# Gate sums beside the output gate tiles only, and the sums of a scan's outputs ten steps later

## The chip, the cores and the metric

The kernel runs on one core of one Trainium2 chip. The metric is the device time of one execution in microseconds. A core has a matrix engine (TensorE, PE in the profile; its weight loads are shown as PEld), VectorE (DVE), ScalarE (ACT), GpSimd (POOL) and a queue engine that issues most transfers (SyncE, SP). Each takes its instructions in the order in which the program gives them, and they wait for each other through semaphores.

## The reference

One decoder layer in float32 for 512 tokens of width 2048: a normalised and conditioned input `h`, one wide projection of it, and two branches that are merged under sigmoid gates. The change lies in the second branch, gated DeltaNet, and in the gate of the conditioning:

```python
mod = jax.nn.silu(c) @ w_ada + b_ada
shift, scale, gate = jnp.split(mod[:, None, :], 3, axis=-1)
...
d_qkv = causal_conv_silu(d_qkv, conv_w)
dq, dk, dv = jnp.split(d_qkv, [DN_KEY, 2 * DN_KEY], axis=-1)
...
o = gated_delta_rule(dq, dk, dv, g, beta)
o = rms_norm(o, dn_norm_w) * jax.nn.silu(dz.reshape(B, T, DN_V_HEADS, DN_HEAD_V).astype(f32))
y_b = o.reshape(B, T, DN_VAL).astype(x.dtype) @ w_o_dn
...
return x + gate * (y @ w_out)
```

There are 16 key heads and 32 value heads, so each key head serves a pair of value heads.

## The kernel before

Float32 products are made of three matmuls: each operand is split into a high part (`hh`, `whi`) and a rest (`hl`, `wlo`), and `mm3` (L250 to L256) adds high by high, rest by high and high by rest. Weights come from memory as `raw` tiles of 1 MB, one per tile of 128 output channels. ScalarE casts half of a tile to `whi` (L52) and VectorE subtracts it to get `wlo` (L53). `channel_tile` runs the 48 matmuls of one such tile, 128 channels by 512 tokens, and calls `pump` after every six of them, eight times in a tile. `pump` is the clock of everything else: a step of each running generator (`live`), of slow paced work, and of side queues, whose entries hold a rate; a side queue adds its rate at every step and moves on by one when it has reached 1. A generator that yields a number sleeps for so many steps. A scheduler then places the instructions on each engine; side work made with `ordered` may not stand before the matmul last issued.

The stage touched is the one of the heads (`heads`, called 16 times by `deltanet`). A head runs five channel tiles: queries `q`, two of values `v`, two of the output gate `z`. Beside them run the short convolution of the tile just finished (`conv`, L591 to L602: on VectorE three multiply-adds, and a last product after a tanh on ScalarE, which writes `yv`), four transposes of `yv` into `ptv`, the products that the scan needs (`pqk`, `py`, `pu`, with `E`, `Y`, `tt` on VectorE), and from the end of the second `v` tile on the scan itself over four chunks (`pv`, `vn`, `vs`, `pd`, `po`, `S`, `pp`, `r`). The scan of head g ends in the first `v` tile of head g + 1. There its result `osb` is scaled and transposed (`pto`), multiplied into the gate tiles `zh` (L1055), and `head_sums` makes four further inputs of 256 columns from the two `zh` tiles, for a product with seven instead of eight multiplications in the next stage. They are written over `osb`; `zh` and they go to memory as the seven slots of `oq_d`. There are two `zh` buffers, so those of head g must have been read out before ScalarE writes the next head's (L880).

Two side queues run through the stage: `od_sums` (rate 0.13 from head 2), sums of weight blocks by a copy on SP and an accumulating transfer on GpSimd of 1 MB each (`od_m`), and, from head 8, `gate` (rate 0.125), which makes the conditioning's gate: 32 steps on VectorE, each over a weight tile `gw` of 0.5 MB, then four small products `pgate`. `gw` has two buffers. Two loads stand ahead, and a step issues the load for the step after next when it has run (L1627 issues, L1636 and L1638 compute). In `branch_b` the slots of `oq_d` are read by the numbers in `od_order`.

Of the kernel before, what the change touches and what calls it, by code (L numbers as in the profile page):

```python
# [7 lines left out]
F32 = mybir.dt.float32  # L8
# [3 lines left out]
ALU = mybir.AluOpType  # L12
# [4 lines left out]
P = 128  # L17
# [19 lines left out]
class Layer:  # L37
# [650 lines left out]

    def od_order(self):
        return [  # L690
            ("m1", 0, (0, 0)), ("m2", 1, (1, 0)), ("m5", 3, None), ("m6", 4, None), ("m7", 5, None), ("m4", 2, None),
            ("m3", 6, (1, 1)),
        ]

# [173 lines left out]
    def heads(self, wk, g):  # L868

        st = {"z": []}  # L870
        self.go(self.queries(wk, g, self.channel_tile(f"q{g}"), st), 0)
        for e in range(2):
            self.go(self.values(wk, g, e, self.channel_tile(f"v{2 * g + e}"), st), 0)
        for e in range(2):
            self.go(self.zgate(wk, self.channel_tile(f"z{2 * g + e}"), st), 0)

# [101 lines left out]
    def scan(self, wk, g, k, kT, TT, qd, M, epsq, st):  # L978
# [3 lines left out]
        osb = wk.tile([P, 2, NTB, P], F32, tag="osb", name="osb", bufs=1)  # L982
        osq = wk.tile([P, 2, NTB], F32, tag="osq", name="osq")
        S = None
        for c in range(NTB):
            if c:
# [3 lines left out]
                for e in range(2):  # L990
                    nc.vector.scalar_tensor_tensor(  # L991
                        out=r[:, e, :], in0=pp[:, e, :], scalar=self.neg_eg[:, c, 2 * g + e : 2 * g + e + 1],
                        in1=v[e][:, c, :], op0=ALU.mult, op1=ALU.add,
# [8 lines left out]
            if c < NTB - 1:  # L1002
                vs = wk.tile([P, 2, P], F32, tag="vs", name="vs", bufs=1)
                for e in range(2):
                    nc.vector.tensor_scalar(
                        out=vs[:, e, :], in0=vn[:, e, :], scalar1=self.kd[:, c, 2 * g + e : 2 * g + e + 1],
# [15 lines left out]
            if c < NTB - 1:  # L1022
# [3 lines left out]
                else:  # L1026
                    for e in range(2):
                        nc.vector.scalar_tensor_tensor(
                            out=Sn[:, e, :], in0=S[:, e, :], scalar=self.egl[:, c, 2 * g + e : 2 * g + e + 1],
                            in1=pd[:, e, :], op0=ALU.mult, op1=ALU.add,  # L1030
# [4 lines left out]
        z = st["z"]  # L1035
# [4 lines left out]
        for e in range(2):  # L1040
            nc.vector.scalar_tensor_tensor(
                out=ms[:, e, :], in0=osq[:, e, :], scalar=1.0 / P, in1=epsq, op0=ALU.mult, op1=ALU.add
# [3 lines left out]
        for e in range(2):  # L1046
            of = osb[:, e]
            nc.vector.tensor_tensor(
                out=of, in0=of, in1=ro[:, e * NTB : (e + 1) * NTB].unsqueeze(2).to_broadcast([P, NTB, P]), op=ALU.mult
            )  # L1050
        yield 2
        for e in range(2):
# [1 line left out]
            self.transpose4(pt, lambda c: osb[:, e, c, :])  # L1054
            nc.vector.tensor_tensor(out=z[e], in0=pt, in1=z[e], op=ALU.mult)  # L1055
            yield 1
        yield from self.head_sums(g, z, osb.rearrange("p e c i -> p (e c i)").rearrange("p (q t) -> p q t", q=4))

    def head_sums(self, g, z, s):

        nc = self.nc
        TT, STT = nc.vector.tensor_tensor, nc.vector.scalar_tensor_tensor
        lo, hi = slice(0, 256), slice(256, 512)
        TT(out=s[:, 0], in0=z[0][:, hi], in1=z[1][:, hi], op=ALU.subtract)
        STT(out=s[:, 1], in0=s[:, 0], scalar=-1.0, in1=z[0][:, lo], op0=ALU.mult, op1=ALU.subtract)
        TT(out=s[:, 2], in0=z[0][:, lo], in1=z[0][:, hi], op=ALU.add)
        STT(out=s[:, 3], in0=s[:, 1], scalar=-1.0, in1=z[1][:, lo], op0=ALU.mult, op1=ALU.subtract)
        yield 4
        for q, src in ((slice(0, 1), z[0][:, lo].unsqueeze(1)), (slice(1, 3), z[1].rearrange("p (q t) -> p q t", q=2)), (slice(3, 7), s)):
            nc.sync.dma_start(out=self.oq_d[q, g // 2].rearrange("q p k t -> p q k t")[:, :, g % 2, :], in_=src)  # L1070


# [659 lines left out]
```

## Time and profile before

| | us |
|---|---|
| median of 3 runs | 2903.31 |
| lowest and highest | 2899.71, 2905.08 |
| profiled execution, own time | 2895.94 |
| its span, first to last instruction | 2894.2 |
| VectorE busy in the span | 1872.6 |
| ScalarE busy in the span | 1138.7 |
| GpSimd busy in the span | 278.9 |

The profile is of one execution, which was 7.4 us below the median. Durations are read from it, and the stage of the heads lies between about 556 and 1586 us of its span. A "releaser" in a row is the event that ended an engine's idle time.

### The profile page before, as it was taken

How to read it: one execution, taken by the hardware profiler on the slowest of the kernel's cores; microseconds unless marked ns; L12 is line 12 of the kernel's file. 1: busy time of each engine (PE TensorE's matmuls, PEld its weight loads, DVE VectorE, ACT ScalarE, POOL GpSimd, SP SyncE). 2: the span in 40 equal slices, each digit the busy share in tenths (PEclk: the TensorE clock that was granted, in tenths of full speed). 3: DMA queues.
4: the chain of work that ended last, by engine and by line, in shares of the span. 5: the costliest groups of instructions: out<-in, count | busy, mean ns of one | idle time of the engine just before them, and what ended most of it. 6: DMA issues, size and time to landing. Idle time of an engine off the chain costs nothing.

```text
span 2894.2 us, 38268 instructions
## 1 busy us (share of the span) xinstructions
PE 2832.6 (98%) x14428; PEld 2322.2 (80%) x14428; DVE 1872.6 (65%) x3020; ACT 1138.7 (39%) x2161; POOL 278.9 (10%) x266
## 2 busy tenths in 40 slices
PE   8899999999999999999999999999999999999999
PEld 6677888888888888888877888888887878788777
DVE  6765899777887556666665456665555655554565
ACT  4354333433334333333333354443343434432343
POOL 0012111101111111111110000000100100000010
PEclk9999999999999999999999999999999999999999
DMA  9756554637667777878772377675745647365575
GB/s 383 291 165 202 171 182 145 209 118 229 190 194 215 236 217 239 240 223 244 247 216 92 127 250 264 245 252 193 224 148 162 176 152 216 108 240 181 182 235 151
DMA packets 205472, 590.08 MB, mean 204 GB/s; under 512 B 74564, under 2 KB 99652, under 8 KB 154088
## 3 DMA queue, kind: packets, MB, share of 16 engines
q1 hardware_dynamic: 195080, 529.44, 53.7%
q0 software_dynamic: 10208, 58.20, 10.3%
q8 instruction: 113, 1.85, 0.3%
q14 instruction: 71, 0.58, 0.1%
HBM read 523.79 MB, written 166.40 MB: 238 GB/s over the span
## 4 chain that ended last, share of the span: by engine, by line
PE 82%; DVE 4%; issue 4%; DMA 2%; ACT 1%; POOL 0%; SPq 0%; DVEq 0%; POOLq 0%; ACTq 0%
PE mm L254 19%; PE mm L256 19%; PE mm L255 19%; PE od L255 3%; PE od L254 3%; PE od L256 3%; PE m L255 1%; PE m L256 1%; PE m L254 1%; PE S L1369 1%; DVE wlo L53 1%; PE pv L998 1%; PE po L1017 1%; PE pP L288 1%; PE O L1420 1%
## 5 line engine op out<-in xcount | busy, mean ns | idle before, releaser
L254 PE MATMUL mm<-hh,whi 128*128 128x512 f32 x2784 | 1133.2, 407 | 2.4 <-ACT whi L52 1.6
L256 PE MATMUL mm<-hh,wlo 128*128 128x512 f32 x2784 | 1090.1, 392 | 1.2 <-DVE wlo L53 1.2
L255 PE MATMUL mm<-hl,whi 128*128 128x512 f32 x2784 | 1087.9, 391 | 0.0
L53 DVE TENSOR_TENSOR wlo<-raw,whi 128x1024 fp32r<-128x1024 f32 (+1 forms) x476 | 591.7, 1246 | 412.7 <-ACT whi L52 403.2
L52 ACT CAST whi<-raw 128x1024 fp32r<-128x1024 f32 (+1 forms) x476 | 495.2, 1044 | 800.6 <-PE mm L255 677.5
L256 PEld LDWEIGHTS mm<-hh,wlo 128*128 128x128 f32 x2784 | 522.9, 188 | 115.3 <-DVE wlo L53 2.1
L254 PEld LDWEIGHTS mm<-hh,whi 128*128 128x128 f32 x2784 | 524.0, 188 | 112.9 <-issue 9.6
L255 PEld LDWEIGHTS mm<-hl,whi 128*128 128x128 f32 x2784 | 524.5, 188 | 99.6 <-issue 1.4
L255 PE MATMUL od<-wlo,oh 128*128 128x512 f32 x448 | 174.6, 390 | 1.0 <-DVE wlo L53 1.0
L254 PE MATMUL od<-whi,oh 128*128 128x512 f32 x448 | 174.9, 391 | 0.0
L256 PE MATMUL od<-whi,ol 128*128 128x512 f32 x448 | 174.4, 389 | 0.0
L945 POOL TENSOR_TENSOR qe<-qe,yq 128x512 f32<-128x512 f32 x32 | 51.0, 1614 | 873.0 <-DMA qe<-eg_rows 504.3
L792 POOL TENSOR_TENSOR E<-E,neg_g 128x512 f32<-128x512 f32 x64 | 87.0, 1359 | 479.1 <-DMA E<-g_rows 332.7
L844 DVE TENSOR_TENSOR A<-A,atmp 128x62 f32<-128x62 f32 (+30 forms) x124 | 112.6, 908 | 1.5
L837 DVE TENSOR_TENSOR atmp<-A 128x62 f32<-128x62 f32 (+30 forms) x124 | 109.2, 881 | 1.4
L255 PEld LDWEIGHTS od<-wlo,oh 128*128 128x128 f32 x448 | 84.1, 188 | 18.5 <-DVE wlo L53 1.3
L256 PEld LDWEIGHTS od<-whi,ol 128*128 128x128 f32 x448 | 84.1, 188 | 17.6
L254 PEld LDWEIGHTS od<-whi,oh 128*128 128x128 f32 x448 | 84.1, 188 | 17.4 <-ACT whi L52 0.4
L53 DVE TENSOR_TENSOR wlo<-raww,whi 128x1024 fp32r<-128x1024 f32 x56 | 68.3, 1222 | 41.1 <-ACT whi L52 41.1
L52 ACT CAST whi<-raww 128x1024 fp32r<-128x1024 f32 x56 | 58.9, 1054 | 76.7 <-PE m L256 66.3
L991 DVE SCALAR_TENSOR_TENSOR r<-pp,neg_eg,vt 128x128 f32<-128x128 f32 x96 | 29.2, 345 | 77.9 <-PE pp L988 77.6
L1393 ACT ACTIVATE sm<-sm,mx,rs 128x256 f32<-128x256 f32 (+1 forms) x128 | 71.7, 561 | 3.3 <-DVE mx L1388 3.3
(341 smaller groups left out, 3274.8 us busy)
## 6 DMA issues: line engine op xcount, KB each, us to landing
raw<-in_w_ch SPq DMA_DIRECT2D x158, 1024.0 KB
wa<-in_w_ada_ss SPq DMA_DIRECT2D x32, 1024.0 KB
od_m<-in_w_od POOLq DMA_DIRECT2D x32, 1024.0 KB, 13.7
raw<-od_m SPq DMA_DIRECT2D x32, 1024.0 KB
raw<-in_w_od SPq DMA_DIRECT2D x24, 1024.0 KB
E<-g_rows SPq DMA_DIRECT2D x64, 256.0 KB
od_m<-in_w_od SPq DMA_DIRECT2D x16, 1024.0 KB
od_m<-od_m SPq DMA_DIRECT2D x16, 1024.0 KB
```

Of the source, the lines that this page charges most:

```text
L52: self.nc.scalar.copy(out=hi, in_=src)
L53: self.nc.vector.tensor_tensor(out=lo, in0=src, in1=hi.bitcast(F32), op=ALU.subtract)
L254: nc.tensor.matmul(ps, lhsT=wh, rhs=xh, start=first, stop=False)
L255: nc.tensor.matmul(ps, lhsT=wh, rhs=xl, start=False, stop=False)
L256: self.last_mm = nc.tensor.matmul(ps, lhsT=wl, rhs=xh, start=False, stop=last).ins
L288: self.nc.tensor.transpose(dst[:, c * P : (c + 1) * P], src_cols(c), self.ident)
L792: self.in_turn(nc.gpsimd.tensor_tensor(out=E, in0=E, in1=ng, op=ALU.add))
L837: eng.tensor_tensor(out=t, in0=A[:, m : m + 1, m + 1 :].to_broadcast([P, m, n]), in1=A[:, :m, m : m + 1].to_broadcast([P, m, n]), op=ALU.mult,
L844: eng.tensor_tensor(out=A[:, :m, m + 1 :], in0=A[:, :m, m + 1 :], in1=t, op=ALU.add)
L945: self.in_turn(nc.gpsimd.tensor_tensor(out=qf, in0=qf, in1=q, op=ALU.mult))
L991: nc.vector.scalar_tensor_tensor(out=r[:, e, :], in0=pp[:, e, :], scalar=self.neg_eg[:, c, 2 * g + e : 2 * g + e + 1], in1=v[e][:, c, :], ...
L1393: nc.scalar.activation(t, t, AF.Exp, scale=r[:, h : h + 1], bias=mx[:, h : h + 1], accum_out=den[:, h : h + 1])
```

## The change

Three things are changed. While a head's `q` and `v` tiles run, the entry of the side queue `gate` has rate 0, and 0.34 while the two `z` tiles run (and after the last head). After the last product with `zh`, a scan sleeps for ten steps, and then makes its sums; between the first two and the last two it sleeps for one more. Three of the sums go to a tile of their own, `zs`, and the fourth over the half of the first `zh` tile that no slot needs any more. The slots are written in three transfers of two, two and three instead of one, two and four, and `od_order` has the new slot numbers.

```diff
-            ("m1", 0, (0, 0)), ("m2", 1, (1, 0)), ("m5", 3, None), ("m6", 4, None), ("m7", 5, None), ("m4", 2, None),
+            ("m1", 0, (0, 0)), ("m2", 2, (1, 0)), ("m5", 4, None), ("m6", 5, None), ("m7", 1, None), ("m4", 3, None),
             ("m3", 6, (1, 1)),
...
         st = {"z": []}
+        for q in self.side.get("gate", []):
+            q[1] = 0.0
         self.go(self.queries(wk, g, self.channel_tile(f"q{g}"), st), 0)
         for e in range(2):
             self.go(self.values(wk, g, e, self.channel_tile(f"v{2 * g + e}"), st), 0)
+        for q in self.side.get("gate", []):
+            q[1] = 0.34
         for e in range(2):
             self.go(self.zgate(wk, self.channel_tile(f"z{2 * g + e}"), st), 0)
...
-        yield from self.head_sums(g, z, osb.rearrange("p e c i -> p (e c i)").rearrange("p (q t) -> p q t", q=4))
+        yield 10
+        yield from self.head_sums(wk, g, z)
...
+        s = wk.tile([P, 3, 256], F32, tag="sums", name="zs", bufs=1)
         TT(out=s[:, 0], in0=z[0][:, hi], in1=z[1][:, hi], op=ALU.subtract)
         STT(out=s[:, 1], in0=s[:, 0], scalar=-1.0, in1=z[0][:, lo], op0=ALU.mult, op1=ALU.subtract)
-        TT(out=s[:, 2], in0=z[0][:, lo], in1=z[0][:, hi], op=ALU.add)
-        STT(out=s[:, 3], in0=s[:, 1], scalar=-1.0, in1=z[1][:, lo], op0=ALU.mult, op1=ALU.subtract)
-        yield 4
-        for q, src in ((slice(0, 1), z[0][:, lo].unsqueeze(1)), (slice(1, 3), z[1].rearrange("p (q t) -> p q t", q=2)), (slice(3, 7), s)):
+        yield 1
+        TT(out=z[0][:, hi], in0=z[0][:, lo], in1=z[0][:, hi], op=ALU.add)
+        STT(out=s[:, 2], in0=s[:, 1], scalar=-1.0, in1=z[1][:, lo], op0=ALU.mult, op1=ALU.subtract)
+        yield 3
+        two = lambda x: x.rearrange("p (q t) -> p q t", q=2)
+        for q, src in ((slice(0, 2), two(z[0])), (slice(2, 4), two(z[1])), (slice(4, 7), s)):
             nc.sync.dma_start(out=self.oq_d[q, g // 2].rearrange("q p k t -> p q k t")[:, :, g % 2, :], in_=src)
```

What this does to the order of the engines is seen at three places of head 10. On TensorE the heads' matmuls, transposes and products keep their places; only the four `pgate` move. New lines stand 4 to 8 lower in the file (L1055 is L1059, L602 stays).

The first place is VectorE while the first `v` tile's convolution runs: `yv` is the tile that the transposes `ptv` wait for, `zh<-pto` the products with the gate tiles, rows that write `osb` or `zs` from `zh` the sums. Before (the gate step L1638 stands one row ahead of the first of these):

```order
L1048 TENSOR_TENSOR osb<-osb,roy 128x512
L913 TENSOR_SCALAR epsq<-ss 128x4
L595 SCALAR_TENSOR_TENSOR yv<-mm,convh,yv 128x511
L53 TENSOR_TENSOR wlo<-raw,whi 128x1024
L595 SCALAR_TENSOR_TENSOR yv<-mm,convh,yv 128x510
L1055 TENSOR_TENSOR zh<-pto,zh 128x512
L595 SCALAR_TENSOR_TENSOR yv<-mm,convh,yv 128x509
L1066 TENSOR_TENSOR osb<-zh 128x256
L1055 TENSOR_TENSOR zh<-pto,zh 128x512
L53 TENSOR_TENSOR wlo<-raw,whi 128x1024
L1064 TENSOR_TENSOR osb<-zh 128x256
L602 SCALAR_TENSOR_TENSOR yv<-th,yv 128x512
```

The same place in the changed kernel:

```order
L53 TENSOR_TENSOR wlo<-raw,whi 128x1024
L595 SCALAR_TENSOR_TENSOR yv<-mm,convh,yv 128x511
L595 SCALAR_TENSOR_TENSOR yv<-mm,convh,yv 128x510
L595 SCALAR_TENSOR_TENSOR yv<-mm,convh,yv 128x509
L1059 TENSOR_TENSOR zh<-pto,zh 128x512
L602 SCALAR_TENSOR_TENSOR yv<-th,yv 128x512
L1059 TENSOR_TENSOR zh<-pto,zh 128x512
L53 TENSOR_TENSOR wlo<-raw,whi 128x1024
L1070 TENSOR_TENSOR zs<-zh 128x256
L1071 SCALAR_TENSOR_TENSOR zs<-zs,zh 128x256
L1073 TENSOR_TENSOR zh<-zh 128x256
L1074 SCALAR_TENSOR_TENSOR zs<-zs,zh 128x256
```

`yv` (L602) now stands ahead of the second product with `zh`, of one `wlo` and of all sums, and no gate step is near. The sums stand behind that `wlo`, and not ten steps lower: nothing holds them to a matmul.

The second place is VectorE in the two `z` tiles of head 10, from the end of the second convolution into the scan. Before:

```order
L602 SCALAR_TENSOR_TENSOR yv<-th,yv 128x512
L53 TENSOR_TENSOR wlo<-raw,whi 128x1024
L966 TENSOR_TENSOR tt_4606<-pu,neg_beta 64x4x64
L966 TENSOR_TENSOR tt_4608<-pu,neg_beta 64x4x64
L1638 SCALAR_TENSOR_TENSOR gate_bc<-gw,silu_c,gate_bc 128x1024
L53 TENSOR_TENSOR wlo<-raw,whi 128x1024
L884 SCALAR_TENSOR_TENSOR zh<-zth,zh 128x512
L1005 TENSOR_SCALAR vs<-vn,kd 128x128 x2
L1025 COPY S<-pd 128x256
L53 TENSOR_TENSOR wlo<-raw,whi 128x1024
L991 SCALAR_TENSOR_TENSOR r<-pp,neg_eg,vt 128x128 x2
L1638 SCALAR_TENSOR_TENSOR gate_bc<-gw,silu_c,gate_bc 128x1024
```

In the changed kernel, where two gate steps stand further ahead, one between `E` and `Y` and one before `tt`:

```order
L970 TENSOR_TENSOR tt_4606<-pu,neg_beta 64x4x64
L970 TENSOR_TENSOR tt_4608<-pu,neg_beta 64x4x64
L602 SCALAR_TENSOR_TENSOR yv<-th,yv 128x512
L53 TENSOR_TENSOR wlo<-raw,whi 128x1024
L1646 SCALAR_TENSOR_TENSOR gate_bc<-gw,silu_c,gate_bc 128x1024
L53 TENSOR_TENSOR wlo<-raw,whi 128x1024
L888 SCALAR_TENSOR_TENSOR zh<-zth,zh 128x512
L1646 SCALAR_TENSOR_TENSOR gate_bc<-gw,silu_c,gate_bc 128x1024
L1009 TENSOR_SCALAR vs<-vn,kd 128x128 x2
L1029 COPY S<-pd 128x256
L53 TENSOR_TENSOR wlo<-raw,whi 128x1024
L1646 SCALAR_TENSOR_TENSOR gate_bc<-gw,silu_c,gate_bc 128x1024
```

Heads 10 and 12 have six gate steps in this order; two steps with loads issued in these same tiles stand ahead of `vs`. Heads 9 and 11 have five, and head 13 nearly so: one such step ahead of `vs`, and one between `vs` and `S`. Head 8 has four: the first two take loads issued in these tiles.

The third place is SP at the end of the second `v` tile and in the `z` tiles of head 10. Before:

```order
L1070 DMA oq_d<-osb 128x4x256
L1627 DMA gw<-in_w_ada_gate 128x1024
L932 DMA ta<-ta_d 64x4x64
L933 DMA lab<-lab_d 64x256
L710 DMA od_m_78<-od_m_77 128x2048
L932 DMA ta<-ta_d 64x4x64
L214 DMA raw<-in_w_ch 128x2048
L933 DMA lab<-lab_d 64x256
L935 DMA ts_11267<-ts_d 64x4x64
L1627 DMA gw<-in_w_ada_gate 128x1024
L214 DMA raw<-in_w_ch 128x2048
L1627 DMA gw<-in_w_ada_gate 128x1024
```

In the changed kernel:

```order
L1078 DMA oq_d<-zs 128x3x256
L936 DMA ta<-ta_d 64x4x64
L1635 DMA gw<-in_w_ada_gate 128x1024
L710 DMA od_m_78<-od_m_77 128x2048
L1635 DMA gw<-in_w_ada_gate 128x1024
L214 DMA raw<-in_w_ch 128x2048
L1635 DMA gw<-in_w_ada_gate 128x1024
L937 DMA lab<-lab_d 64x256
L936 DMA ta<-ta_d 64x4x64
L937 DMA lab<-lab_d 64x256
L1635 DMA gw<-in_w_ada_gate 128x1024
L939 DMA ts_11274<-ts_d 64x4x64
```

Four loads of `gw` stand in this stretch where there were three, none ahead of `ta`, and two follow within the next two tiles.

More of the change, by code (lines that the diff above doesn't have):

```diff
@@ L1056, in scan, with head_sums @@
             yield 1
-        yield from self.head_sums(g, z, osb.rearrange("p e c i -> p (e c i)").rearrange("p (q t) -> p q t", q=4))
-    def head_sums(self, g, z, s):
+        yield 10
+        yield from self.head_sums(wk, g, z)
+    def head_sums(self, wk, g, z):
         nc = self.nc
```

## The prediction, made before the changed kernel ran

> **What bounds the kernel now.** I read the page first, then TensorE's idle time and its waits in the stage of the heads, then the timeline around one of them. The page says that the matrix engine sets the end:
>
> ```profile
> span 2894.2 us, 38268 instructions
> PE 2832.6 (98%) x14428; PEld 2322.2 (80%) x14428; DVE 1872.6 (65%) x3020; ACT 1138.7 (39%) x2161; POOL 278.9 (10%) x266
> ```
>
> So only time in which TensorE stands idle can be won. The second view cuts the stage's heads 7 to 14 where TensorE loads the first weights of `pqk`; its columns are the stretch and its length, then busy time of PE, PEld, DVE, ACT and POOL, the granted clock, the DMA engines' share and GB/s:
>
> ```profile
> 1027.40:1094.70 67.30, 67.30 (x357) 56.03 (x356) 37.27 (x70) 25.01 (x56) 4.22 (x5) 1.00 0.78 236
> 1094.70:1168.00 73.30, 69.53 (x366) 57.49 (x365) 49.81 (x75) 24.77 (x56) 17.46 (x17) 1.00 0.79 224
> ...
> sum 558.40, PE 544.82 PEld 450.69 DVE 342.27 ACT 199.81 POOL 71.85; mean PE 68.10 PEld 56.34 DVE 42.78 ACT 24.98 POOL 8.98
> ```
>
> The first row has a single gate step, close to its end, and no idle time. All eight hold 558.40 - 544.82 = 13.6 us of it, and are 558.4 - 8 x 67.3 = 20.0 us longer than eight such stretches. What ended TensorE's waits from 1100 to 1620 us, with total, times and longest:
>
> ```profile
> PE ptv L288 <- DVE yv L602: 10.0, 5, 2.6
> PE pto L288 <- DVE zh L1055: 2.2, 1, 2.2
> PE pu L963 <- DVE Y L959: 1.4, 1, 1.4
> ```
>
> All of the 13.6 us is VectorE being late. The timeline of VectorE and TensorE at one such wait, in the first `v` tile of head 9 (start, length, engine):
>
> ```profile
> 1155.21 0.69 DVE L1048 TENSOR_TENSOR osb<-osb,roy 128x512 f32<-128x512 f32 x1
> 1155.82 1.28 DVE L1638 SCALAR_TENSOR_TENSOR gate_bc<-gw,silu_c,gate_bc 128x1024 f32<-128x1024 f32 x1
> 1157.01 1.80 DVE L1048 TENSOR_TENSOR osb<-osb,roy 128x512 f32<-128x512 f32 x1
> ...
> 1165.65 1.21 DVE L53 TENSOR_TENSOR wlo<-raw,whi 128x1024 fp32r<-128x1024 f32 x1
> 1167.12 0.68 DVE L602 SCALAR_TENSOR_TENSOR yv<-th,yv 128x512 f32<-128x512 f32 x1
> 1168.51 1.28 DVE L1638 SCALAR_TENSOR_TENSOR gate_bc<-gw,silu_c,gate_bc 128x1024 f32<-128x1024 f32 x1
> ...
> 1167.95 0.95 PE L288 MATMUL ptv<-ident,yv 128*128 128x128 f32 x4 [2.38 <-DVE yv L602]
> ```
>
> From `osb` on `yv` takes 12.6 us, and TensorE had come to `ptv` 2.38 us before. The same place in the head without gate sums:
>
> ```profile
> 1019.04 1.29 DVE L1048 TENSOR_TENSOR osb<-osb,roy 128x512 f32<-128x512 f32 x2
> 1024.53 1.15 DVE L602 SCALAR_TENSOR_TENSOR yv<-th,yv 128x512 f32<-128x512 f32 x1 [0.16 <-ACT th L600]
> 1029.23 0.60 PE L288 MATMUL ptv<-ident,yv 128*128 128x128 f32 x4
> ```
>
> There `yv` takes 6.6 us, and 3.5 us are left over.
>
> **What the change takes away.** In the `v` tiles of heads 9 to 15 VectorE's rows become those of the head without gate sums, with `yv` ahead of every sum. So the five waits of `ptv` (10.0), that of `pu` (1.4, a gate step ahead of `Y` in head 8; its steps now stand behind `tt`) and that of `pto` (2.2, in head 15, where no gate work is left at that place) should all go: -13.6 us. Bounds: all of it, since the same rows left 3.5 us over; and nothing, if something that I don't see holds `yv`.
>
> Part of the clock was lost there too. Stretches of 10 us, with the columns as above:
>
> ```profile
> 1160.00:1170.00 10.00, 7.62 (x35) 6.05 (x34) 9.76 (x13) 2.27 (x3) 6.25 (x7) 0.91 0.94 182
> 1170.00:1180.00 10.00, 10.00 (x71) 7.96 (x70) 5.88 (x9) 3.31 (x4) 0.00 (x0) 0.92 1.03 261
> 1180.00:1190.00 10.00, 10.00 (x50) 8.31 (x49) 5.01 (x8) 3.08 (x5) 0.00 (x0) 1.00 1.07 350
> 1190.00:1200.00 10.00, 10.00 (x50) 8.37 (x49) 4.28 (x6) 3.98 (x10) 0.00 (x0) 1.00 0.92 331
> 1200.00:1210.00 10.00, 10.00 (x52) 8.45 (x51) 4.09 (x11) 3.29 (x9) 0.00 (x0) 1.00 0.14 37
> ```
>
> 10 x 0.09 + 10 x 0.08 = 1.7 us at full speed, around the wait of 2.38 us: -1.7. Of the 20.0 us, 4.7 are neither idle time nor clock; the products `pgate`, which stay, are part of it, and I count none of it as won.
>
> The Trainium skill (TensorE: Matmul & The Clock Gate, section Part 1) has the clock halve only after an idle window of about 3.4 us. Here it fell at a wait of 2.38 us, so the measurement decides; by the page this fall would not hang on the wait, and the gain would be 1.7 us smaller.
>
> **What it adds.** No instruction, and no byte. But the gate's loads are drawn together. A step issues the load for the step after next. Before, steps were 12.7 us apart (1155.82 to 1168.51), and no wait of VectorE for `gw` stands in its list of waits. Now the third step in a pair of `z` tiles takes a load that the first issued in the same tiles, when the DMA engines are fullest. Follow the bytes in head 9, by GpSimd's and SP's issues:
>
> ```profile
> 1159.90 1.68 POOL L714 DMA_DIRECT2D od_m<-in_w_od  x2
> 1163.91 0.51 SPq L710 DMA_DIRECT2D od_m<-od_m  x1
> 1165.58 0.82 POOL L714 DMA_DIRECT2D od_m<-in_w_od  x1
> 1166.89 0.33 SPq L214 DMA_DIRECT2D raw<-in_w_ch  x1
> 1168.62 0.37 SPq L1070 DMA_DIRECT2D oq_d<-osb  x1
> 1175.83 2.76 SPq L932 DMA_DIRECT2D ta<-ta_d  x1
> 1185.60 0.34 SPq L214 DMA_DIRECT2D raw<-in_w_ch  x1
> ```
>
> In the new order the first load stands behind `ta`, so at 1178.6 or later. Ahead of it since 1160 are five transfers of 1.05 MB, the slots (0.92) and `ta` and `lab` (0.1), 6.3 MB; with its own 0.5 MB, 6.8. The last column of the stretches (GB/s) gives 1.8, 4.4, 7.9 and 11.2 MB moved by 1170, 1180, 1190 and 1200. So the load lands near 1186.8 (an estimate), and VectorE, which has run the second step by 1182 or so, stands until then. Behind that step in its queue are `wlo`, `zh`, `vs`, `S` and `r`, for which the scan on TensorE waits:
>
> ```profile
> 1187.52 0.68 DVE L884 SCALAR_TENSOR_TENSOR zh<-zth,zh 128x512 f32<-128x512 f32 x1
> 1189.11 0.49 DVE L1005 TENSOR_SCALAR vs<-vn,kd 128x128 f32<-128x128 f32 x2 [0.91 <-ACT vn L1000]
> 1191.25 0.60 PE L1013 MATMUL pd<-vs,k 128*128 128x256 f32 x2
> 1194.91 0.59 PE L988 MATMUL pp<-S,kT 128*128 128x256 f32 x2
> ```
>
> In heads 9, 11 and 13: step until 1188.1 (1.28), `wlo` (1.2) 1189.3, `zh` 1190.0, `vs` 1190.5. `pd` comes at 1191.25: nothing lost, 0.7 us left. The next step's load lies behind the `raw` of 1185.60 (8.5 MB, near 1191.7); that step ends at 1193.0, ahead of `S` for `pp` at 1194.9: nothing lost. In heads 10 and 12 a second such step stands ahead of `vs`. In head 10 its load lies behind a copy of 1.05 MB: 8.4 MB, near 1191.4, step until 1192.7, `vs` 1193.2, `pd` 1.9 us late; in head 12 there is no copy, and `pd` is late by about 0.6. Head 8 takes two fresh loads, two rows earlier. Together some 2.5 us. Below: 0, if the engines drain sooner. Above: each MB more ahead of a load costs 1 / 0.331 = 3.0 us, which in six heads comes to 14 to 18. With 0.7 us of margin in three heads I take 5, nearer to the rows than to the bound.
>
> The sums move by less than ten steps, into time when VectorE waits for the next `wlo`, whose row stands here with ScalarE's next write of the first `zh`:
>
> ```profile
> 1172.15 1.22 DVE L53 TENSOR_TENSOR wlo<-raw,whi 128x1024 fp32r<-128x1024 f32 x1 [2.35 <-ACT whi L52]
> 1186.25 0.68 ACT L880 ACTIVATE zh<-mm,dnwh 128x512 f32<-128x512 f32 x1
> ```
>
> 2.35 us of idle time cover them: cost 0; without the cover `E` and then `Y` for `pu` would be about 2 us later in each head. By the bytes above a slot issued by 1169 is read out of `zh` by about 1182, 4 us ahead of that write: cost 0, at most 1 us a head. The new slot numbers move no byte.
>
> **The sum.** -13.6 - 1.7 + 5 = -10.3. Against the profiled execution that is 2895.9 - 10.3 = 2885.6; the median of the runs stands 7.4 us above that execution, so I say 2903.3 - 10.3 = 2893.0 us. Its own range goes from -16 to -4: 2887 to 2899.
>
> **The rivals.** (1) *VectorE stops for `gw`.* One mechanism: a gate step at the head of VectorE's queue waits for its load, and holds `vs` and `S` behind it. It decides once the third step's load lands after 1187.5, since then `pd` is late in every head; that is 0.7 us past my estimate. For it: the DMA engines' share is over 0.9 from 1160 to 1200, and the page has 13.7 us from issue to landing for GpSimd's transfers, which share the engines:
>
> ```profile
> od_m<-in_w_od POOLq DMA_DIRECT2D x32, 1024.0 KB, 13.7
> ```
>
> A load issued at 1178.6 would land at 1192.3; the step ends at 1193.6, `wlo`, `zh` and `vs` at 1196.0, and `pd` is 4.8 us late. Over six heads 29 us, less the 15.3 won: +13, 2917 us. Against it: a late TensorE gives the loads more time, and before VectorE never waited for one. (2) *Everything goes and nothing comes:* the loads land as they are wanted, and some of the 4.7 us goes too: -15 to -20, 2885 us. For it: the share falls to 0.14 behind the `z` tiles, so there is room in a head as a whole. (3) *No net change:* new waits in the `z` tiles as large as those removed in the `v` tiles, some 2 us in each of seven heads: 2903 us.
>
> **How the numbers follow.** Forecast 0.42, (1) 0.32, (2) 0.11, (3) 0.15. A change under 0.2%, 5.8 us, can't be told from none here. 0.40 of the forecast's 0.42 is over that, with (2) 0.51 faster; (3) and small parts of the forecast and of (1) make 0.18 the same; 0.31 slower. The range reaches to the edges of (2) and (1), until no more than 0.2 is left out: 2882 to 2916.
>
> **What would show it.** TensorE's waits of `ptv` for `yv` near 0 in the heads, and stretches of about 67.3 us. If the forecast holds, a short wait of `pd` for `vs` in head 10, and VectorE idle ahead of L1646 for a few us with `gw` as the releaser. If (1) holds, waits of `pd` or `pp` for `vs` and `S` in every head with fresh loads, 3 us or more each. If `ptv` still waits for `yv`, the account of the gain is wrong.

## The result, and the profile after

| | before | after |
|---|---|---|
| median of 6 runs each, us | 2902.90 | 2925.73 |
| lowest and highest, us | 2899.71, 2905.08 | 2920.60, 2930.89 |
| ratio, with its 95% interval | | 1.0086, 1.0074 to 1.0098 |
| profiled execution, us | 2895.94 | 2930.89 |
| its span, us | 2894.2 | 2929.1 |

The change makes the kernel 0.9% slower. The forecast was 2893.0 us with a range of 2882 to 2916, so both its sign and its range were wrong. What happened is the first rival, priced at 2917.

The first view of the kernel after is the stage cut at the first weights of `pqk`, heads 7 to 14 as in the prediction. (The prediction's own cuts lie some 3 us ahead of these weights: the first stands at 1030.8 in the kernel before, not at 1027.4. Cut at the weights, its eight stretches give the same 558.4 and 544.8 us. And the stage doesn't end at about 1586 us: the last head runs on to about 1650.)

```profile
1034.40:1101.70 67.30, 67.30 (x357) 56.03 (x356) 37.02 (x67) 25.14 (x56) 7.21 (x8) 1.00 0.72 212
1101.70:1176.50 74.80, 70.40 (x357) 57.78 (x356) 42.12 (x72) 24.80 (x56) 10.91 (x11) 0.95 0.76 231
1176.50:1251.40 74.90, 70.40 (x357) 58.17 (x356) 43.23 (x72) 25.04 (x56) 8.88 (x8) 0.95 0.75 216
1251.40:1320.10 68.70, 67.53 (x357) 55.95 (x356) 44.84 (x76) 25.04 (x56) 8.55 (x9) 1.00 0.79 242
1320.10:1393.10 73.00, 69.06 (x358) 57.14 (x357) 43.01 (x73) 24.92 (x56) 10.08 (x10) 0.98 0.76 226
1393.10:1470.20 77.10, 70.21 (x358) 58.00 (x357) 43.84 (x72) 25.03 (x56) 7.26 (x8) 0.93 0.72 225
1470.20:1549.40 79.20, 69.53 (x357) 57.55 (x356) 41.58 (x71) 25.83 (x58) 10.46 (x10) 0.94 0.65 181
...
sum 586.10, PE 555.17 PEld 458.31 DVE 337.57 ACT 199.78 POOL 65.94; mean PE 69.40 PEld 57.29 DVE 42.20 ACT 24.97 POOL 8.24
```

The eight stretches take 586.1 us against 558.4, 27.7 more. TensorE is idle for 586.1 - 555.2 = 30.9 us (before 13.6), and the rest above eight times 67.3 is 586.1 - 538.4 - 30.9 = 16.8 us (before 20.0 - 13.6 = 6.4). So 17.3 us of the loss are idle time and 10.4 are busy time that got longer, in the stretches whose clock column fell to 0.93 to 0.98. The spans differ by 34.9 us; of the other 7.2, 2.5 lie ahead of the heads, 1.1 in heads 0 to 6, where only the sums and the slots have moved, and 3.6 behind head 14. The medians differ by only 22.8: the profiled execution of before is faster than all of its six runs, and that of the kernel after is the slowest of its six.

What ended TensorE's waits from 1100 to 1700 us (total, times, longest):

```profile
PE pd L1017 <- DVE vs L1009: 26.9, 6, 9.7
PE pp L992 <- DVE S L1029: 3.7, 1, 3.7
PE pto L288 <- DVE osb L1052: 1.3, 1, 1.3
PE pu L968 <- DVE gate_bc L1656: 0.3, 1, 0.3
```

VectorE's waits for the gate's loads from 1020 to 1640 us, of the same kernel:

```profile
DVE gate_bc L1646 <- DMA gw<-in_w_ada_gate: 56.8, 12, 11.5
DVE gate_bc L1644 <- DMA gw<-in_w_ada_gate: 7.0, 1, 7.0
```

The waits of `ptv` for `yv` are gone, as forecast. In their place the scan's `pd` and `pp` wait 30.6 us for `vs` and `S` (4.4, 4.5, 1.2, 3.9, 6.9 and 9.7 us in heads 8 to 13), and VectorE, which never waited for `gw` before, now waits 63.8 us for it. The timeline of head 9 joins the two. VectorE's rows (start, length):

```profile
1187.46 1.27 DVE L1646 SCALAR_TENSOR_TENSOR gate_bc<-gw,silu_c,gate_bc 128x1024 f32<-128x1024 f32 x1
1197.81 1.29 DVE L1646 SCALAR_TENSOR_TENSOR gate_bc<-gw,silu_c,gate_bc 128x1024 f32<-128x1024 f32 x1 [9.08 <-DMA gw<-in_w_ada_gate]
1200.15 0.69 DVE L888 SCALAR_TENSOR_TENSOR zh<-zth,zh 128x512 f32<-128x512 f32 x1
1200.75 0.48 DVE L1009 TENSOR_SCALAR vs<-vn,kd 128x128 f32<-128x128 f32 x2
```

SP's issues there:

```profile
1182.55 5.50 SPq L1635 DMA_DIRECT2D gw<-in_w_ada_gate  x1
1188.11 0.69 SPq L936 DMA_DIRECT2D ta<-ta_d  x1
```

And TensorE's late product:

```profile
1201.28 1.22 PE L1017 MATMUL pd<-vs,k 128*128 128x256 f32 x2 [4.50 <-DVE vs L1009]
```

The second step ends at 1188.7 and the third stands at the head of VectorE's queue for 9.08 us. Its load went to SP at 1182.55, where the one issue took 5.50 us, and had landed at 1197.8, 15.3 us after the issue began. `vs`, behind it, makes `pd` 4.50 us late.

The clock around that stall, in stretches of 2 us (columns as in the prediction, the clock third from the end):

```profile
1195.00:1197.00 2.00, 1.78 (x8) 1.13 (x6) 0.00 (x0) 0.54 (x2) 0.00 (x0) 1.00 1.20 233
1197.00:1199.00 2.00, 0.00 (x0) 0.00 (x0) 1.19 (x1) 0.64 (x1) 0.00 (x0) 1.00 0.97 349
1199.00:1201.00 2.00, 0.00 (x0) 0.00 (x0) 2.00 (x5) 0.00 (x0) 0.00 (x0) 0.92 0.96 383
1201.00:1203.00 2.00, 1.72 (x6) 1.54 (x7) 0.83 (x3) 0.00 (x0) 0.00 (x0) 0.50 0.60 227
1203.00:1205.00 2.00, 2.00 (x7) 1.61 (x7) 2.00 (x3) 1.01 (x5) 0.00 (x0) 0.50 0.20 39
1205.00:1207.00 2.00, 2.00 (x7) 1.52 (x6) 1.34 (x2) 0.00 (x0) 0.00 (x0) 0.50 0.82 274
1207.00:1209.00 2.00, 2.00 (x9) 1.68 (x8) 0.45 (x2) 0.00 (x0) 0.00 (x0) 0.87 0.83 342
```

TensorE stops at 1196.8 and goes on at 1201.28. The clock falls to half near 1200.7 and stays there for some 6 us of work, until about 1207.5, which costs about 3 us more: a stall of 4.5 us is a loss of about 7.5. Not every stall does this: behind the 1.17 us of head 10 the clock stays at 1.00.

The theory from this is **A**: a gate step waits at the head of VectorE's queue for a load that was issued in the same two tiles, and holds the scan; the longer stalls, from 3.7 us on here, also cost clock. Its rivals are **B**, that the later sums, their tile or the slots lose the time, and **C**, that the steps' own time on VectorE does, whatever the loads do. Within A it is open why the loads are late.

### The profile page after: what moved, and what is told of

It reads as the page before. It is cut to its first block, busy times and chain, and to the rows that moved or that the text cites. A ratio compares the mean times of both kernels' runs of the same rounds, so it can differ in the third digit from the quotient of the medians.

```text
span 2929.1 us, 38248 instructions
## 1 busy us (share of the span) xinstructions
PE 2849.6 (97%) x14428; PEld 2334.1 (80%) x14428; DVE 1867.9 (64%) x3020; ACT 1139.5 (39%) x2161; POOL 273.4 (9%) x266
## 4 chain that ended last, share of the span: by engine, by line
PE 82%; DMA 4%; issue 3%; DVE 2%; ACT 0%; SPq 0%; POOL 0%; DVEq 0%; POOLq 0%; ACTq 0%
PE mm L254 20%; PE mm L256 19%; PE mm L255 19%; PE od L255 3%; PE od L254 3%; PE od L256 3%; DMA gw<-in_w_ada_gate 3%; PE m L255 1%; PE m L256 1%; PE m L254 1%; PE S L1377 1%; PE po L1021 1%; PE O L1428 1%; PE pv L1002 1%; PE pP L288 1%
## 5 line engine op out<-in xcount | busy, mean ns | idle before, releaser
L1646 DVE SCALAR_TENSOR_TENSOR gate_bc<-gw,silu_c,gate_bc 128x1024 f32<-128x1024 f32 x30 | 38.4, 1279 | 56.8 <-DMA gw<-in_w_ada_gate 56.8
```

The costliest lines, as they stand in the source:

```text
L1646: nc.vector.scalar_tensor_tensor(out=o, in0=ws.pop(i), scalar=s, in1=o, op0=ALU.mult, op1=ALU.add)
```

## Experiments

| run | gate steps in | other edit | median, us | ratio to before, 95% |
|---|---|---|---|---|
| e1_gate_only | z | old sums | 2927.5 | 1.0083 to 1.0113 |
| e2_sums_only | all, 0.125 | new sums | 2893.6 | 0.9975 to 0.9994 |
| e4_no_loads | z | 30 of 32 loads left out | 2882.4 | 0.9924 to 0.9957 |
| e5_q_and_z | q and z | | 2888.0 | 0.9953 to 0.9979 |
| e6_slots_early | z | slots in earlier heads | 2913.9 | 1.0034 to 1.0072 |
| e7_q_z_slots_early | q and z | slots in earlier heads | 2913.4 | 1.0038 to 1.0072 |
| e8_more_in_q | 3 in q, 2 in z | | 2881.8 | 0.9920 to 0.9964 |
| e9_q_only | q | | 2882.3 | 0.9922 to 0.9966 |
| e10_act_queue | z | loads issued by ScalarE | 2912.0 | 1.0033 to 1.0056 |
| e10b_pool_queue | z | loads issued by GpSimd | 2889.3 | 0.9956 to 0.9976 |
| e11_q_only_old_sums | q | old sums | 2881.9 | 0.9916 to 0.9959 |

The kernel before ran beside them at 2897.6 to 2898.1 us (medians of the three groups of runs). Where nothing else is said, a kernel is the changed one with the edit shown.

### Which part of the change loses the time

e1 puts only the new rates into the kernel before; e2 takes only the rates out of the kernel after.

```diff
 e1, to the kernel before
+        for q in self.side.get("gate", []):
+            q[1] = 0.0
         self.go(self.queries(wk, g, self.channel_tile(f"q{g}"), st), 0)
...
+        for q in self.side.get("gate", []):
+            q[1] = 0.34
 e2, to the kernel after: these four lines taken out
```

> The kernel before with one part of the change: the gate's steps stand only beside z tiles (0 in q and v, 0.34 in z). Slot numbers, the sums' place and their tile are as before. Theory A (VectorE stands at the head of its queue for a gate load that was issued in the same two tiles; TensorE then waits for vs and S, and its clock falls after such waits): most of the loss is here, 2915 to 2930 us against 2903 before, with waits of VectorE at L1646's counterpart for gw of 40 us or more in all and waits of pd and pp of 20 to 35 us. Rival B (the ten steps' delay, the sums' own tile or the new slot numbers cost the time): within 6 us of before, or faster by the 13.6 us of waits removed.

> The changed kernel with the gate's rate left at 0.125 through all tiles, so that only the slot numbers, the ten steps' delay and the tile of three sums are left of the change. Theory A: no wait of VectorE for gw; the time is that of before or up to 8 us less (2895 to 2905), since yv then stands ahead of the sums; what is left of the waits of ptv is the gate steps' share. Rival B: 2915 us or more, waits at zh's next write or at the slots.

e1 is 1.0098 against 1.0086 for the whole change: the rates alone lose it all. TensorE's waits in e1, 1020 to 1640 us:

```profile
PE pd L1017 <- DVE vs L1009: 29.8, 5, 10.0
PE pp L992 <- DVE S L1029: 3.0, 1, 3.0
```

They are nearly those of the kernel after. In e2, over the same time:

```profile
PE ptv L288 <- DVE yv L602: 6.2, 4, 2.6
PE pto L288 <- DVE zh L1055: 2.2, 1, 2.2
PE pu L963 <- DVE Y L959: 2.0, 2, 1.3
```

e2 is faster than before by 0.16%, at 2893.6 us a little below the range of A: with the sums out of the way the waits of `ptv` fall from 10.0 to 6.2 us, and none of TensorE's waits is for the slots or for `zh`'s next write. B falls. VectorE waits for `gw` once, 1.6 us, where A expected nothing.

### Is it the loads or the steps

```diff
         for i in range(2 * KT):
...
+            w = ws.pop(i)
...
-                nc.vector.scalar_tensor_tensor(out=o, in0=ws.pop(i), scalar=s, in1=o, op0=ALU.mult, op1=ALU.add)
+                nc.vector.scalar_tensor_tensor(out=o, in0=w, scalar=s, in1=o, op0=ALU.mult, op1=ALU.add)
             if i + 2 < 2 * KT:
-                load(i + 2)
+                ws[i + 2] = w
```

> The changed kernel in which the gate's steps read the first two loaded pieces again and again: every VectorE instruction of the steps stays, at the same place, and 30 of the 32 loads of 0.52 MB are left out (so the gate's values are not those of the reference). Theory A: the waits of VectorE for gw (63.8 us) go, those of pd and pp for vs and S fall from 31 us to under 3, the clock stays at 1.00 from 1100 to 1700, and the time is 2880 to 2895 us. Rival C (the steps' own 1.28 us on VectorE, five or six of them beside the scan, make vs and S late, whatever the loads do): waits of pd and pp of 15 us or more remain and the time stays over 2910.

All that is left of TensorE's waits in the stage (1040 to 1640 us):

```profile
PE pto L288 <- DVE osb L1052: 1.3, 1, 1.3
PE pd L1017 <- DVE vs L1009: 0.5, 1, 0.5
```

Every VectorE instruction of the steps is still there, beside the scan, and the time is 2882.4 us. C falls, and A holds in size: with the loads gone the changed kernel is 0.6% faster than before.

### Fewer steps beside the scan

```diff
+            q[1] = 0.21
         self.go(self.queries(wk, g, self.channel_tile(f"q{g}"), st), 0)
+        for q in self.side.get("gate", []):
+            q[1] = 0.0
...
-            q[1] = 0.34
+            q[1] = 0.21
```

> The changed kernel with the gate's steps in three tiles of a head in place of two: rate 0.21 in q and z tiles, 0 in v tiles, so 1.7 steps a tile and about 8 us between two steps. Theory A: a load issued in a z tile lands 14 to 20 us later, which is two to two and a half steps away; only the steps in the second z tile meet a load that has not landed, and they wait 2 to 6 us. VectorE's waits for gw fall from 63.8 to 15 to 35 us, and the time lies between 2890 and 2912. Rival C: it depends on the number of steps beside the scan alone, 3.4 in place of 5.4 a head: 2905 to 2918, without VectorE waiting for gw first.

VectorE's waits for `gw` in e5:

```profile
DVE gate_bc L1648 <- DMA gw<-in_w_ada_gate: 21.4, 8, 9.1
```

And TensorE's longest group:

```profile
PE pp L994 <- DVE S L1031: 5.5, 2, 5.3
```

The waits for `gw` are a third of the change's, and 2888.0 us is a little better than A's range. The longest of them, 9.1 us, is above the 2 to 6 us that A expected.

### Why the loads are late

e6 and e7 make the slots of the od sums earlier (e7 with e5's rates); e8 and e9 move the steps into `q` tiles.

```diff
 e6 and e7
-                        self.beside(self.ordered(self.od_sums()), 0.13, "ws")
+                        self.beside(self.ordered(self.od_sums()), 0.29, "ws")
 e8: rates 0.36 in q, 0.0 in v, 0.14 in z
 e9: rates 0.64 in q, 0.0 in v, 0.0 in z
```

> The changed kernel with the slots of the od sums (copies of 1.05 MB on SP's queue, accumulating adds on GpSimd's) made in the earlier heads: their rate is 0.29 in place of 0.13 from head 2 on, so that they end near head 8 and none is left beside the gate's loads; the gate's steps stay in the z tiles alone. A1 (the gate's loads land late because the engines and the queue are full of the slots' transfers at that time): VectorE's waits for gw fall from 63.8 us to under 25 and the time to 2885 to 2902. A2 (they land late because each is issued only two steps ahead, behind the transfers that the head itself needs, ta, lab, ts and raw): the waits stay at 40 us or more and the time over 2912. A cost of its own: earlier heads may wait for their weights, up to 10 us.

> The gate's steps in q and z tiles at 0.21 (2888 us, VectorE's waits for gw 21.4 us, TensorE's for S 5.5 us) and the slots made in the earlier heads as well. A1: the waits for gw go to under 8 us, that of TensorE to under 1, and the time to 2880 to 2885. A2: no change beyond 3 us, 2885 to 2891. If the earlier heads can't take the slots' transfers: 2892 or more, with waits for whi or wlo in heads 2 to 8.

In e6 VectorE doesn't wait for `gw` at all in heads 8 to 15, with the steps in the `z` tiles as in the change. SP's issues of `gw` (shortest, median and longest time of one, in ns) in the kernel after:

```profile
L1635 SPq DMA_DIRECT2D gw<-in_w_ada_gate x32: 327/328/6117, 1107.7 to 1503.1; - x32
```

The same group in e6:

```profile
L1635 SPq DMA_DIRECT2D gw<-in_w_ada_gate x32: 327/328/577, 1135.7 to 1486.5; - x32
```

Without the slots' transfers the longest issue is 0.58 us, not 6.12: A1, the traffic, is shown as a condition of the waits (on the engines or on SP's queue, which e6 does not tell apart). The close spacing is the other condition: in e2 the slots are there, the steps are far apart, and the waits are 1.6 us. The time of e6, 2913.9 us, misses A1's range and is above the kernel before, because the slots now crowd other heads. TensorE's waits in e6 from 880 to 1140 us:

```profile
PE pd L1017 <- DVE vs L1009: 18.9, 1, 18.9
PE ptv L288 <- DVE tt L970: 5.9, 1, 5.9
```

A wait of ScalarE's in that time:

```profile
ACT atmp L849 <- DMA ta_d<-atmp: 22.6, 4, 16.2
```

VectorE's and TensorE's rows behind that wait, which ends at 937.86 and is followed by another of 5.3 us:

```profile
946.28 1.22 DVE L53 TENSOR_TENSOR wlo<-raw,whi 128x1024 fp32r<-128x1024 f32 x1 [22.55 <-ACT whi L52]
947.42 0.48 DVE L1009 TENSOR_SCALAR vs<-vn,kd 128x128 f32<-128x128 f32 x2
947.95 1.22 PE L1017 MATMUL pd<-vs,k 128*128 128x256 f32 x2 [18.92 <-DVE vs L1009]
```

The stretch from `pqk` to `pqk` around it, from 898.7 to 987.8, takes 89.1 us instead of 67.3. ScalarE stands there for transfers of `ta_d`, its next `whi` starts only at 945.21, VectorE's `wlo` waits 22.55 us for it, `vs` stands behind `wlo`, and `pd` is 18.92 us late. The expected cost of up to 10 us was too small. e7 has the same loss, a wait of `pd` of 20.0 us, and no wait for `gw` either: its time is the third case of its expectation, though TensorE waits for `vs`, not for weights.

> The changed kernel with 0.36 in q tiles, 0 in v, 0.14 in z: three steps in a q tile, where the DMA engines' share falls to 0.14, and two in a pair of z tiles, whose loads were issued in the q tile 30 us before. A2: no step beside the scan meets a fresh load; VectorE's waits for gw come in q tiles only, where TensorE has nothing that waits for VectorE within 5 us; pd and pp wait under 2 us in all, time 2880 to 2888. A1: loads of the z tiles land in time too, the same. Rival D (the queue order in q matters: a step that waits there holds wlo, and TensorE waits for weights): 2890 or more, with waits of mm for wlo.

> The changed kernel with all of the gate's steps in q tiles (0.64 there, 0 elsewhere): five steps 2.7 us apart, so each load is issued only 5 us before its step, nearer than in the z tiles of the change. A2 (the short lead alone makes the loads late): VectorE waits for gw in every q tile, 30 us or more in all; A1 (the full engines do): a load of 0.52 MB lands within 4 to 8 us there, the waits are 2 to 4 us a step at most and 10 to 30 us in all, and since no scan stands behind them in q, TensorE loses under 5 us: 2882 to 2892.

In e9 the steps around 1200 us follow each other by 1.5 to 6 us, so a load is issued only two such gaps ahead. VectorE's waits for `gw` in e9:

```profile
DVE gate_bc L1648 <- DMA gw<-in_w_ada_gate: 9.4, 10, 2.0
```

Its eight stretches, the second and the sum:

```profile
1099.90:1167.20 67.30, 67.30 (x357) 56.03 (x356) 44.70 (x73) 24.71 (x56) 11.11 (x10) 1.00 0.82 244
...
sum 543.00, PE 542.94 PEld 450.14 DVE 340.10 ACT 200.08 POOL 67.94; mean PE 67.87 PEld 56.27 DVE 42.51 ACT 25.01 POOL 8.49
```

The waits are 9.4 us in ten, none longer than 2.0 (a little less than even A1 expected), and TensorE stands idle for 0.06 us in eight stretches: A2, the short lead by itself, falls. (The expectation was wrong that no scan stands behind the steps in `q`: its `vs` and `S` run there too, but a wait of 2 us doesn't reach TensorE.) e8 has no wait for `gw` and the same time. Both are as fast as e4, which leaves 30 of the loads out, so nothing of the gate's loads is left on the path; both beat the kernel before and the one after.

The last three ask whether SP's queue holds the loads, and what the later sums are worth in the best place.

```diff
-            nc.sync.dma_start(out=ws[i], in_=a["w_ada_gate"]...
+            nc.scalar.dma_start(out=ws[i], in_=a["w_ada_gate"]...
 e10b: nc.gpsimd.dma_start
 e11, to the kernel before: e9's rates
```

> The changed kernel with the gate's loads issued by ScalarE in place of SP, so that they stand in no line behind ta, lab, ts and raw and don't wait for SP's queue to go on (in the changed kernel single issues of a gate load take 5.50 us and more there, against 0.33 otherwise). L1 (the line on SP's queue is what makes them late): landing within 8 us of the issue, VectorE's waits for gw under 25 us, time 2885 to 2905. L2 (the sixteen engines themselves are full, whatever queue a load comes by): waits of 40 us or more, time 2912 to 2935. ScalarE's own order has a cost in either: an issue that waits for a gate step holds whi behind it.

> The same with the loads issued by GpSimd, which holds nothing that TensorE waits for at that place but has the accumulating adds of the slots ahead in its queue. L1: VectorE's waits for gw fall below 40 us; time 2890 to 2912. L2: 50 us or more, 2915 to 2935.

> The kernel before with the gate's steps in q tiles alone (0.64 there, 0 elsewhere), and none of the rest of the change: old slot numbers, sums right behind the scan, in its own tile. It tells what the later sums are worth once the gate's steps are out of their way. If the later sums win anything beside that, this is slower than 2882 by 2 us or more, with waits of ptv for yv; if the gate's steps alone had made yv late, it is 2880 to 2884 and the later sums are worth nothing.

VectorE's waits for `gw` in e10:

```profile
DVE gate_bc L1646 <- DMA gw<-in_w_ada_gate: 32.1, 11, 5.9
```

What TensorE waits for most there:

```profile
PE pv L1002 <- ACT vt L899: 17.4, 5, 10.1
```

VectorE's waits for `gw` in e10b:

```profile
DVE gate_bc L1646 <- DMA gw<-in_w_ada_gate: 14.4, 7, 4.0
```

And the time from issue to landing that the trace has for its `gw` transfers:

```profile
DMA to landing us min/median/max: 4.0/6.7/12.1
```

From ScalarE's queue the waits are 34.5 us (32.1, and 2.4 of the first step) against 63.8: nearly half went with the line on SP's queue and the rest stayed, so neither L1 nor L2 holds alone (and TensorE's own stops give the loads some time). That line is seen in the kernel after: the second step of head 9 ends at 1188.7, and the load that it makes room for goes to SP only at 1195.13, behind `ta`, `lab`, `ts` and `raw`. The time of e10 is no good, since ScalarE now stands for gate steps itself and `vt` behind it holds `pv`: around 1186 it is idle for 8.43 us, issues a load 0.1 us after a gate step has ended, and goes on with `vt`. From GpSimd's queue they are 14.4 us and the kernel is faster than before; but there the accumulating adds of the slots stand behind the loads and move too (ahead of its loads GpSimd waits 149 us in all for gate steps), so this run doesn't separate the line from the traffic. e11 ends at 2881.9 us: with the steps in `q`, the later sums are worth nothing (e9 is 2882.3).

## Why the prediction was wrong

- **What bounds the kernel, and -13.6.** Right. The five waits of `ptv`, that of `pu` for `Y` and that of `pto` for `zh` went. (The 1.3 us of `pto` for `osb` stand behind 1640 us in both kernels, outside the prediction's list.) e8, e9 and e11 win 2898 - 2882 = 16 us, near the second rival's 15 to 20. The reason was half right: `yv` needs the gate's steps out of the `v` tiles, and the sums need not move.
- **-1.7 for the clock.** The fall in the `v` tile went, but no term stood for the clock after the new waits. The part of the stage that is neither idle time nor the plain stretch rose from 6.4 to 16.8 us. That the fall hung on the length of the wait is not shown: a wait of 2.64 us at 1514.4 in the kernel before left the clock at 1.00.
- **+5 for VectorE's wait.** This is the step that failed, at its sentence "`pd` comes at 1191.25: nothing lost, 0.7 us left". The 1191.25 is a row of the kernel before, where TensorE comes to `pd` of head 9 only after the wait of 2.38 us and the slow clock, and the prediction books both as gone (-2.4 in the -13.6, and -1.7). So the deadline had to move up by some 4 us, and in the working it did not. The two executions don't run at the same times, so both are counted here from the issue of the first two `od_m` transfers, at 1159.90 before and here in the kernel after:

```profile
1169.31 1.68 POOL L714 DMA_DIRECT2D od_m<-in_w_od  x2
```

  | in head 9, us after that issue | reckoned | measured |
  |---|---|---|
  | the third step's load is issued | 18.7 | 13.2, and the issue ends at 18.7 |
  | it has landed | 26.9 | 28.5 |
  | TensorE comes to `pd` | 31.4 | 27.5 |
  | `pd` can run | 30.6 | 32.0 |

  So the load landed 1.6 us later than reckoned, and TensorE came to `pd` 3.9 us sooner: 0.7 us to spare became a stop of 4.5. (In heads 10 to 12 TensorE comes to `pd` 26.8 to 29.0 us after that issue in the kernel before already.) The count of the bytes held. The engines' rows of the kernel after are:

```profile
1160.00:1170.00 10.00, 10.00 (x54) 8.42 (x53) 7.29 (x18) 4.82 (x17) 3.23 (x4) 1.00 0.91 310
1170.00:1180.00 10.00, 10.00 (x54) 8.40 (x53) 9.14 (x13) 3.80 (x5) 6.34 (x7) 1.00 0.98 209
1180.00:1190.00 10.00, 10.00 (x72) 7.83 (x71) 7.48 (x11) 2.07 (x3) 0.00 (x0) 1.00 0.99 250
1190.00:1200.00 10.00, 6.78 (x32) 5.33 (x30) 2.19 (x2) 3.63 (x6) 0.00 (x0) 1.00 1.08 286
```

  From 1169.3 to 1197.8 the last column gives 0.2 + 2.1 + 2.5 + 2.2 = 7.0 MB, where 6.8 were reckoned. The issue that stood for 5.50 us cost nothing against the reckoning in this head, since it had begun 5.5 us sooner. The other heads were not reckoned well either: head 10 was to be latest, by 1.9 us, and was late by 1.2; heads 11 and 13 were to lose nothing and lost 3.9 and 9.7. These were not followed load by load, so how their stops divide between landing and deadline stays open.
- **The sums, the slots and the `zh` buffers at 0.** Right: e2 loses nothing. (Once in the kernel after, ScalarE's write of `zh` waits 2.0 us for a slot; none of TensorE's waits stands behind it.)
- **Rival (1), +13, 2917 us.** Its mechanism was right. That its size was right too, 29 us of idle time priced for six heads and 30.6 measured, was luck: the stops go from 1.2 to 9.7 us, and in head 9 its 4.8 us come near the 4.5 because a landing that was 3.9 us too late (32.4 us in the count above) stood against a deadline that was 3.9 us too late. Of its price 10.4 us of longer busy time were missing; with them it is 29 - 13.6 + 10.4 = 25.8 us, and the medians differ by 22.8. It had 0.32 because the forecast's landing stood 0.7 us inside a margin; with the deadline put right the forecast's own numbers make `pd` some 3 us late.

The Trainium skill (DMA: Bandwidth & Descriptors, section Issuing engines are not separate DMA queues) says that transfers of all issuing engines share the same 16 DMA engines, and that another issuer saves only the time to initiate, which it calls usually small. The waits left in e10, 34.5 us, fit the first half. On SP's queue that time was not small here: single issues took up to 6.12 us, and 29.3 us of the waits went in e10.

## What to carry to other kernels

Side work with a prefetch of two buffers has to be spread so that a step comes later than its load can land where it is placed: ask for each step when its load is issued, what is in flight then, and who stands behind the step in its engine's queue. Take the deadline from the order that the change leaves: where the change removes a delay of the engine that waits, that engine also comes sooner to what may be late. If the same number of steps has a place where the transfers are few, as the `q` tiles here, a close spacing does no harm. Price a new stall of several us with its clock as well, and where a landing is within a few us of the deadline, let the bound decide the chance.

## What the runs showed that was not expected

An issue of a gate load on SP's queue, 0.33 us as a rule, took up to 6.12 us in the kernel after. It took at most 0.58 us in e6, without the slots' transfers, and in e9, with them but with the steps in the `q` tiles; what holds an issue was not traced. The kernel before has issues of 2.75 and 4.91 us too, and no step there waits. A load of 0.5 MB landed 15.3 us after its issue began in the full `z` tiles, and the loads from GpSimd's queue 4.0 to 12.1 us after theirs. TensorE's clock, once it had fallen near 1200.7, 4 us into an idle time of 4.5, stayed at half until about 1207.5, so that the clock cost about two thirds as much again as this stall.
